# Gate rows of the mLSTM heads: requested in the projection stage of their pair

## The chip, the cores and the metric

The kernel runs on one core of a Trainium2 chip. The metric is the device time of one execution in microseconds (us), as a median over runs. The core's engines are TensorE (PE, matrix multiplies and transposes; its weight loads are shown as PEld), VectorE (DVE), ScalarE (ACT), GpSimd (POOL) and SyncE (SP). Each works through its own queue in order and waits on semaphores for the others. All loads and stores of this kernel are issued by SP and carried out by 16 DMA engines.

## What is computed

Two layers of a bidirectional encoder run over two request groups of 256 and 512 tokens with shared weights, width 1024. Each layer has a mixer stage with three groups of heads (A: dilated attention, 4 heads; B: mLSTM, 4 heads; C: grouped-query attention, 8 heads), a cross attention into 256 memory tokens, and a gated FFN with a convolution. The part that matters here is B. Cut down, and for one direction:

```
g  = gates of the head                      # input gate ig, forget gate lf = log_sigmoid(...)
b  = cumsum(lf)                             # over the tokens
logw[l, s] = b[l] - b[s] + ig[s]            # s <= l (forward); the backward scan has s >= l
w_intra = exp(logw - m[l]) * (q[l] . k[s])
h[l] = sum_s w_intra v[s] / max(|sum_s w_intra|, exp(-m[l]))
```

The kernel computes each mLSTM head as a full attention within its stream: for a block of 128 queries it needs, along the keys, the row `ig - b` of the forward and of the backward direction, the same for all queries. These are the gate rows. They are added to a triangular mask in the diagonal block, put through an exponential with a bias by query, and multiplied with the scores.

## The kernel before, in words

Activations are kept transposed, features on the 128 partitions and the 768 tokens of both streams along the free axis (`T` = 768; `STREAMS` is first tokens 256 to 767, then 0 to 255). Values are float32, split into a high and a low float32r part for the matrix multiplies. A large buffer `f_all` (`arena_f` in the rows), `F_COLS` = 14 x 768 = 10752 float32 columns, is handed out in pieces by an `Arena`: it gives the columns that have been free for longest, and the tile framework makes a new user of columns wait for the last user. `arena_r` is the same for float32r values. Softmax tiles (`palloc`, 512 columns each) and nearly all intermediate results of a mixer stage come from `arena_f`.

In the mixer stage (`mixers`) each head group has a projection (`c_q`, `b_proj`, `a_proj`) and an attention (`c_attn`, `b_attn`, `a_attn`). The helper `ahead(first, second)` writes the projection of the next group with a low priority and the attention of the present one with a high priority, so that a scheduler fills the attention's gaps with the next projection. The scheduler sets the order in every engine's queue when the program is built. The order of the groups is C (two groups of four heads), B (two pairs of heads, `pb` = 0 and 1), A (two pairs).

`gates` computes the gate rows of all four B heads and both directions in 36 partitions and stores them to DRAM (`scr_g`, line 560). `b_proj(pb)` projects the pair's queries and keys, convolves them, stacks them by DMA (`stacks`, line 362) and projects the values (`v_proj`). `b_attn(pb)` goes over the two heads `e` of the pair and the two streams; for each it takes a buffer `gbt` of 2n columns (1024 or 512), loads the two gate rows from `scr_g` into it, repeated over all partitions (line 729), and calls `attend` with the softmax `b_soft`. For each block of 128 queries `b_soft` adds the mask to the diagonal part (DVE, the tile that reads `arena_f,cs`), takes up to four exponentials (ACT, lines 748 to 752) and multiplies them with the scores from PSUM while summing (DVE, line 754); PE's score products (lines 375, 376) refill a PSUM bank that line 754 has read, and its transposes of the weights (line 387) read the softmax tile, after which the tile's columns are free.

There are 16 such gate-row loads: 2 heads x 2 streams x 2 pairs x 2 layers. In the FFN the same `f_all` is split anew: the first 7168 columns hold weight sums, the rest (3584 columns) the working tiles of one step.

Of the kernel before, what the change touches and what calls it, by code (L numbers as in the profile page):

```python
# [30 lines left out]
T = 768  # L31
# [3 lines left out]
STREAMS = ((256, 512), (0, 256))  # L35
# [9 lines left out]
R_COLS = 18 * 768  # L45
S_COLS = 4 * 512
PREP = 7 * 512
F_COLS = 14 * 768
N_PAR = 143

K_ID, K_TRI, K_IND = 0, 128, 384
# [57 lines left out]
def trunk_kernel(ctx, tc, xT, memT, w_in, w_out, w_xq, w_xkv, w_xo, w_up, w_dn, w_dnt, par, fin_g, cst, fmk, tabs,  # L109
                 out_p, out_s):  # L110
    nc = tc.nc
    V, A, G, PE, SY = nc.vector, nc.scalar, nc.gpsimd, nc.tensor, nc.sync
# [12 lines left out]
    ap = ctx.enter_context(tc.tile_pool(name="ap", bufs=1))  # L125
    f_all = ap.tile([128, F_COLS], F32, name="arena_f")
    af = Arena(f_all, F_COLS)
    r_all = ap.tile([128, R_COLS + S_COLS], F32R, name="arena_r")
# [26 lines left out]
    scr_g = nc.dram_tensor("scr_g", (DEPTH, 36, T), F32, kind="Internal").ap()  # L155

    def tt(out, a, b, op):
        V.tensor_tensor(out, a, b, op=op)  # L158

    def stt(out, a, s, b, op0, op1):  # L160
        V.scalar_tensor_tensor(out=out, in0=a, scalar=s, in1=b, op0=op0, op1=op1)  # L161
# [78 lines left out]
    def proj(src, xh, xl, evac, streams=STREAMS, sub="", chunks=None):  # L240
        chunks = chunks or wload8(src, sub)
        for c0, n in streams:
            ps = ps_tile(n)
            mm_chunks(ps[:, :n], chunks, xh, xl, c0, n)
            evac(ps[:, :n], c0, n)
# [76 lines left out]
    def split(src, hi, lo, n, scale=None, sub="sp"):  # L322
        hi_op(pick("h" + sub, "A"), hi[:, :n], src[:, :n], scale)
        if scale is None:
            tt(lo[:, :n], src[:, :n], hi.bitcast(F32)[:, :n], ALU.subtract)
        else:
            stt(lo[:, :n], src[:, :n], scale, hi.bitcast(F32)[:, :n], ALU.mult, ALU.subtract)
# [9 lines left out]
    def v_tokens(zv, nt, vv, site):  # L337
        for c0, n in (STREAMS if nt == 6 else ((0, 512),)):
            ps = small_ps(site, "vps")
            m = n // 128  # L340
            j0 = c0 // 128
            for i in range(m):
                PE.transpose(ps[:, i * 128:(i + 1) * 128], zv[:, c0 + i * 128:c0 + (i + 1) * 128], ident)
            for e in range(2):
                src = ps[:, :n].rearrange("p (i h d) -> p i h d", h=2, d=64)[:, :, e]
                a, b = 64 * e, 64 - 64 * e
                A.copy(vv[e][:, j0:j0 + m, a:a + 64], src)
                tt(vv[e][:, j0:j0 + m, b:b + 64], src, vv[e].bitcast(F32)[:, j0:j0 + m, a:a + 64], ALU.subtract)
# [164 lines left out]
    def mixers(l, xt, x_dram, stats):  # L513
# [7 lines left out]
        def ev_to(z, name):  # L521
            return ev_scaled(z, rbc, name)
# [91 lines left out]
        def v_proj(t):  # L614
            zv = ft()
            proj(w_in[l, t], xh, xl, ev_to(zv, "v%d" % t), sub="w_v%d" % t)
            vv = [rtl(), rtl()]
            v_tokens(zv, 6, [tok(v) for v in vv], "v%d" % t)
            af.free(zv)
            return vv  # L620
# [56 lines left out]
        def stacks(qq, kk):  # L677
            out = []
            qf, kf = qq.bitcast(F32), kk.bitcast(F32)
            for e in range(2):  # L680
                r = slice(64 * e, 64 * e + 64)
                qs, K = rtl(), rtl(2 * T)
                load_stack(qs, [(0, qf[r, :T]), (64, qf[r, T:])])
                load_stack(K, [(0, kf[r]), (64, kf[r])])
                out.append((qs, K))
            ar.free(qq, kk)
            return out

        def b_proj(pb):
            parts = []  # L690
            for j in range(2):
                ti = 6 + 2 * j + pb
                ci = 2 * j + pb
                u = af.tile(771)
                G.memset(u[:, 0:1], 0.0)
                G.memset(u[:, 257:258], 0.0)
                G.memset(u[:, 770:771], 0.0)

                def ev_c(ps, c0, n, u=u):
                    o = c0 + (2 if c0 else 1)  # L700
                    tt(u[:, o:o + n], ps, rbc[:, c0:c0 + n], ALU.mult)
                proj(w_in[l, ti], xh, xl, ev_c, sub="w_b%d%d" % (pb, j))
                t = af.tile(769)
                w = lambda r, ci=ci: pr[:, l, C_BW + 4 * r + ci:C_BW + 4 * r + ci + 1]
                A.activation(t, u[:, 1:770], ACT.Identity, scale=w(1), bias=pr[:, l, C_BB + ci:C_BB + ci + 1])
                stt(t, u[:, 0:769], w(0), t, ALU.mult, ALU.add)
                stt(t, u[:, 2:771], w(2), t, ALU.mult, ALU.add)
                th = af.tile(769)
                A.activation(th, t, ACT.Tanh)
                z = u[:, 0:T]  # L710
                stt(z[:, 0:256], th[:, 0:256], 1.0, t[:, 0:256], ALU.add, ALU.mult)
                stt(z[:, 256:768], th[:, 257:769], 1.0, t[:, 257:769], ALU.add, ALU.mult)
                hl = rtl(2 * T)
                split(z, hl[:, :T], hl[:, T:], T, sub="b_sp%d" % pb)
                af.free(u, t, th)
                parts.append(hl)
            sts = stacks(*parts)
            return sts, v_proj(10 + pb)

        def b_attn(pb, sv):  # L720
            SITE[0] = "b%d" % pb
            sts, vv = sv
            for e in range(2):
                qs, K = sts[e]
                hd = 2 * pb + e
                for c0, n in STREAMS:
                    gbt = af.tile(2 * n)
                    gb = gbt.rearrange("p (d k) -> p d k", d=2)
                    SY.dma_start(out=gb, in_=scr_g[l, hd:hd + 33:32, c0:c0 + n].partition_broadcast(128))
                    attend(qs, c0, n // 128, K[:, :T], K[:, T:], c0, n, tok(vv[e]), c0 // 128, e, yt[5 + pb], c0,  # L730
                           b_soft(gb, c0, n, hd))
                    af.free(gbt)
                ar.free(qs, K, vv[e])

        def b_soft(gb, c0, n, hd):
# [127 lines left out]
        def f1():  # L863
            r = c_q(1)
            gates()
            return r
        qc1 = ahead(f1, lambda: c_attn(0, qc0), "0")
        sb0 = ahead(lambda: b_proj(0), lambda: c_attn(1, qc1), "1")
        sb1 = ahead(lambda: b_proj(1), lambda: b_attn(0, sb0), "2")
        sa0 = ahead(lambda: a_proj(0), lambda: b_attn(1, sb1), "3")  # L870
        def fa():
            r = a_proj(1)
# [98 lines left out]
    def ffn(l, xt, stats):  # L971
        _, rbc = stats
        rf = Arena(r_all, R_COLS + S_COLS, T)
        fp = Arena(f_all[:, :2 * PREP], 2 * PREP)
        fw = Arena(f_all[:, 2 * PREP:], F_COLS - 2 * PREP)
        fs = Arena(f_all[:, PREP:2 * PREP], PREP)
        ftm = Arena(f_all[:, 2 * PREP:], F_COLS - 2 * PREP)
        tg = f_all[:, F_COLS - T:]
        gf = pr[:, l, C_FFN:C_FFN + 8]
# [388 lines left out]
```

## Time and profile before

| | |
|---|---|
| time, median of 3 runs | 2231.02 us (2229.93 to 2237.94) |
| the profiled execution: its time, its span | 2230.71 us, 2228.8 us |
| PE busy, PE weight loads busy | 91%, 81% |
| DVE busy, ACT busy | 86%, 46% |
| mean granted TensorE clock | 0.951 of full speed |
| chain that ended last: PE, DVE, ACT, DMA | 69%, 18%, 5%, 5% |
| mixer stage, first layer: 245 to 300 us | PE 40.06, DVE 43.80 us busy, clock 0.75 |
| mixer stage, first layer: 300 to 350 us | PE 39.94, DVE 39.11 us busy, clock 0.86 |
| mixer stage, second layer: 1320 to 1370 us | PE 38.23, DVE 32.46 us busy, clock 0.90 |
| FFN main loop, first layer: 640 to 1050 us | PE 404.17, DVE 389.01 us busy, clock 1.00 |

A busy PE is not PE at its peak: matrix multiplies overlap in the records. The granted clock is the share of full speed at which the chip let TensorE run; 0.50 is the lower of its two levels, 1.2 of 2.4 GHz. The chain is found by going back from the last instruction, at each step to what released it. A waiting time is idle time of an engine directly before an instruction, put down to the last of the things that it waited for.

### The profile page before, as it was taken

The numbers are of one execution on the slowest core, as the hardware profiler recorded it, in microseconds if no ns is written. First come the engines' busy times: TensorE is split into PE (matmuls) and PEld (weight loads), VectorE is DVE, ScalarE is ACT, GpSimd is POOL, SyncE is SP. The second block draws the span as 40 slices with busy tenths as digits, with TensorE's granted clock in tenths as the row PEclk, the third lists the DMA queues.
The fourth block names the chain that finished last, engine by engine and source line by source line (L and its number), as shares of the span: only waits on it lengthen the run. The fifth ranks groups of instructions, "written<-read, shape, count | busy, mean of one in ns | idle before, by whom it ended". The sixth has DMA issues, their size and how long they took to land.

```text
span 2228.8 us, 31329 instructions
## 1 busy us (share of the span) xinstructions
PE 2036.8 (91%) x11256; PEld 1801.0 (81%) x11256; DVE 1925.8 (86%) x4191; ACT 1031.6 (46%) x2030; POOL 2.3 (0%) x28
## 2 busy tenths in 40 slices
PE   7989788898889999999999897898988999999996
PEld 5877667677769999999888775776867899999995
DVE  8787788778899999999978777878789999999997
ACT  4256645546633333333444675465565333333342
POOL 0000000000000000000000000000000000000000
PEclk8989888899999999999999897999998999999998
DMA  5422341434212222222245133443422222222211
GB/s 202 121 59 71 97 110 48 130 114 119 86 52 86 68 67 75 67 67 69 89 150 139 41 80 89 103 113 121 125 76 66 86 67 67 74 69 66 67 38 67
DMA packets 64684, 195.16 MB, mean 88 GB/s; under 512 B 8264, under 2 KB 11592, under 8 KB 63760
## 3 DMA queue, kind: packets, MB, share of 16 engines
q1 hardware_dynamic: 64528, 193.15, 29.7%
q8 instruction: 89, 1.46, 0.3%
q14 instruction: 67, 0.55, 0.1%
HBM read 150.17 MB, written 10.71 MB: 72 GB/s over the span
## 4 chain that ended last, share of the span: by engine, by line
PE 69%; DVE 18%; ACT 5%; DMA 5%; issue 2%; SPq 1%; DVEq 0%; ACTq 0%
PE rps L1066 9%; PE rps L1068 9%; PE rps L1067 9%; DVE arena_f L158 5%; PE rps L1109 5%; PE rps L1110 4%; PE rps L1111 4%; PE prS L213 4%; PE prS L214 4%; PE prS L215 4%; DVE arena_r L158 2%; PE t L387 2%; PE prP L213 2%; DVE xall L158 2%; DVE arena_f L161 2%
## 5 line engine op out<-in xcount | busy, mean ns | idle before, releaser
L183 ACT CAST wh<-arena_f 128x512 fp32r<-128x512 f32 x280 | 170.7, 620 | 286.3 <-PE rps L1067 231.3
L158 DVE TENSOR_TENSOR arena_f<-arena_f 128x512 f32<-128x512 f32 (+3 forms) x381 | 272.8, 733 | 19.2 <-DMA arena_f<-arena_f 8.4
L183 ACT CAST wh<-wr 128x512 fp32r<-128x512 f32 x268 | 165.0, 620 | 260.3 <-PE rps L1067 105.0
L158 DVE TENSOR_TENSOR wl<-wr,wh 128x512 fp32r<-128x512 f32 x288 | 197.5, 688 | 37.2 <-ACT wh L183 35.5
L1066 PE MATMUL rps<-xha,wh 128*128 128x384 f32 x640 | 218.7, 342 | 7.7 <-DVE arena_f L158 4.5
L1068 PE MATMUL rps<-xha,wl 128*128 128x384 f32 x640 | 213.5, 340 | 6.3 <-DVE wl L158 6.2
L1067 PE MATMUL rps<-xla,wh 128*128 128x384 f32 x640 | 217.6, 340 | 0.1
L158 DVE TENSOR_TENSOR xall<-rps,xall 128x512 f32<-128x512 f32 (+1 forms) x384 | 198.4, 554 | 14.7 <-PE rps L1111 5.6
L1109 PE MATMUL rps<-arena_r,wh 128*128 128x512 f32 (+1 forms) x608 | 202.8, 340 | 1.6 <-DVE xall L158 1.6
L1110 PE MATMUL rps<-arena_r,wh 128*128 128x512 f32 (+1 forms) x608 | 200.9, 338 | 0.0
L213 PE MATMUL prS<-xha,wh 128*128 128x512 f32 x480 | 191.4, 402 | 5.5 <-DVE arena_f L158 1.9
L214 PE MATMUL prS<-xla,wh 128*128 128x512 f32 x480 | 191.6, 400 | 1.3 <-DVE xla L158 1.2
L158 DVE TENSOR_TENSOR wl<-arena_f,wh 128x512 fp32r<-128x512 f32 x280 | 189.7, 687 | 2.5 <-ACT wh L183 2.3
L215 PE MATMUL prS<-xha,wl 128*128 128x512 f32 x480 | 190.5, 398 | 0.0
L158 DVE TENSOR_TENSOR arena_f<-rps,arena_f 128x384 f32<-128x384 f32 x280 | 151.7, 555 | 33.9 <-PE rps L1068 29.9
L1111 PE MATMUL rps<-arena_r,wl 128*128 128x512 f32 (+1 forms) x608 | 177.9, 338 | 0.0
L1066 PE MATMUL rps<-arena_r,wh 128*128 128x384 f32 x480 | 163.0, 340 | 0.8 <-ACT wh L183 0.8
L1067 PE MATMUL rps<-arena_r,wh 128*128 128x384 f32 x480 | 161.9, 337 | 0.0
L1068 PE MATMUL rps<-arena_r,wl 128*128 128x384 f32 x480 | 156.0, 339 | 0.7 <-DVE wl L158 0.7
L158 DVE TENSOR_TENSOR arena_r<-t,arena_r 128x512 fp32r<-128x512 f32 x184 | 125.0, 687 | 27.9 <-ACT arena_r L183 26.6
L213 PE MATMUL prP<-xha,wh 128*128 128x256 f32 x480 | 141.8, 295 | 4.8 <-DVE arena_f L158 1.8
L387 PE MATMUL t<-cs,arena_f 128*128 128x128 f32 x736 | 127.9, 292 | 18.2 <-DVE arena_r L158 8.1
(211 smaller groups left out, 4971.4 us busy)
## 6 DMA issues: line engine op xcount, KB each, us to landing
arena_f<-in_w_up SPq DMA_DIRECT2D x80, 512.0 KB
wr<-in_w_in SPq DMA_DIRECT2D x42, 512.0 KB
wr<-in_w_dn SPq DMA_DIRECT2D x40, 512.0 KB
wr<-in_w_out SPq DMA_DIRECT2D x32, 512.0 KB
arena_r<-arena_r SPq DMA_DIRECT2D x32, 384.0 KB
arena_r<-arena_r SPq DMA_DIRECT2D x48, 192.0 KB
xall<-in_xT SPq DMA_DIRECT2D x8, 768.0 KB
arena_r<-arena_r SPq DMA_DIRECT2D x64, 96.0 KB
```

Source lines behind the costliest of these rows:

```text
L158: V.tensor_tensor(out, a, b, op=op)
L183: A.copy(out, a)
L213: PE.matmul(ps, h[:, j], xh[i][:, c0:c0 + n], start=i == 0, stop=False)
L214: PE.matmul(ps, h[:, j], xl[i][:, c0:c0 + n], start=False, stop=False)
L215: PE.matmul(ps, lo[:, j], xh[i][:, c0:c0 + n], start=False, stop=i == tot - 1)
L387: PE.transpose(t[:, j * n + i * 128:j * n + (i + 1) * 128], ptiles[i][:, (kb + j) * 128:(kb + j + 1) * 128], ident)
L1066: PE.matmul(ps, h[:, k], x[k], start=k == 0, stop=False)
L1067: PE.matmul(ps, h[:, k], x[4 + k], start=False, stop=False)
L1068: PE.matmul(ps, lo[:, k], x[k], start=False, stop=k == 3)
L1109: PE.matmul(ps, h[:, m], hh[i][:, c], start=k == 0 and not tail, stop=False)
L1110: PE.matmul(ps, h[:, m], hlo[i][:, c], start=False, stop=False)
L1111: PE.matmul(ps, lo[:, m], hh[i][:, c], start=False, stop=i == b - 1)
```

## The change

The loads of the gate rows move from `b_attn` to the end of `b_proj` of the same pair. There is one buffer of 2T = 1536 columns for each head, which takes both streams, instead of one buffer for each stream; it is freed when `b_attn` is through with the head. `arena_f` grows from 14 x 768 to 18 x 768 = 13824 columns, and to make room the scratch for dynamic DMA in SBUF is set to 1024 bytes. Shapes, number and sources of the loads and all arithmetic stay as they are.

```diff
@@ -45,7 +45,7 @@
 R_COLS = 18 * 768
 S_COLS = 4 * 512
 PREP = 7 * 512
-F_COLS = 14 * 768
+F_COLS = 18 * 768
 N_PAR = 143
 
 K_ID, K_TRI, K_IND = 0, 128, 384
@@ -715,21 +715,28 @@
                 af.free(u, t, th)
                 parts.append(hl)
             sts = stacks(*parts)
-            return sts, v_proj(10 + pb)
+            vv = v_proj(10 + pb)
+            rows = []
+            for e in range(2):
+                hd = 2 * pb + e
+                gbt = af.tile(2 * T)
+                for c0, n in STREAMS:
+                    gb = gbt[:, 2 * c0:2 * c0 + 2 * n].rearrange("p (d k) -> p d k", d=2)
+                    SY.dma_start(out=gb, in_=scr_g[l, hd:hd + 33:32, c0:c0 + n].partition_broadcast(128))
+                rows.append(gbt)
+            return sts, vv, rows
 
         def b_attn(pb, sv):
             SITE[0] = "b%d" % pb
-            sts, vv = sv
+            sts, vv, rows = sv
             for e in range(2):
                 qs, K = sts[e]
                 hd = 2 * pb + e
                 for c0, n in STREAMS:
-                    gbt = af.tile(2 * n)
-                    gb = gbt.rearrange("p (d k) -> p d k", d=2)
-                    SY.dma_start(out=gb, in_=scr_g[l, hd:hd + 33:32, c0:c0 + n].partition_broadcast(128))
+                    gb = rows[e][:, 2 * c0:2 * c0 + 2 * n].rearrange("p (d k) -> p d k", d=2)
                     attend(qs, c0, n // 128, K[:, :T], K[:, T:], c0, n, tok(vv[e]), c0 // 128, e, yt[5 + pb], c0,
                            b_soft(gb, c0, n, hd))
-                    af.free(gbt)
+                af.free(rows[e])
                 ar.free(qs, K, vv[e])
 
         def b_soft(gb, c0, n, hd):
@@ -1351,7 +1358,7 @@
     from concourse.bass_utils import run_bass_kernel_spmd as _run
 
     a = _layout({k: np.asarray(v) for k, v in inputs.items()})
-    nc = _bacc.Bacc("TRN2", target_bir_lowering=False, num_devices=1)
+    nc = _bacc.Bacc("TRN2", target_bir_lowering=False, num_devices=1, dynamic_dma_scratch_size=1024)
     arrays, args = {}, []
     for name in _ORDER:
         v = np.ascontiguousarray(a[name])
```

The scheduler sets the order anew. Lines behind the edit are 7 higher: the exponentials of lines 748, 749, 750 and 752 are 755, 756, 757 and 759 in the new program, and the gate-row loads are line 725.

SP's queue in the first layer, from the store of the gates (`scr_g<-arena_f`) on; `wr` is a weight tile, `arena_r<-arena_r` a stack load, `arena_f<-scr_g` a gate-row load of pair 0. Before:

```order
L560 DMA scr_g<-arena_f 36x768
L177 DMA wr<-in_w_in 128x1024 x2
L362 DMA arena_r<-arena_r 64x768 x2
L177 DMA wr<-in_w_in 128x1024
L362 DMA arena_r<-arena_r 64x1536 x4
L362 DMA arena_r<-arena_r 64x768 x2
L177 DMA wr<-in_w_in 128x1024 x2
L362 DMA arena_r<-arena_r 64x768 x2
L177 DMA wr<-in_w_in 128x1024
L729 DMA arena_f<-scr_g 128x2x256
L729 DMA arena_f<-scr_g 128x2x512
```

After:

```order
L560 DMA scr_g<-arena_f 36x768
L725 DMA arena_f<-scr_g 128x2x256 x2
L177 DMA wr<-in_w_in 128x1024 x2
L362 DMA arena_r<-arena_r 64x768 x2
L725 DMA arena_f<-scr_g 128x2x512 x2
L362 DMA arena_r<-arena_r 64x1536 x4
L177 DMA wr<-in_w_in 128x1024
L362 DMA arena_r<-arena_r 64x768 x2
```

The four loads of pair 0 moved from behind all projections of the pair to between the store and the pair's stack loads.

SP's queue in the first layer, later. Before, in `b_attn` of pair 1: its gate-row loads, with the stack loads of the first A pair in between:

```order
L729 DMA arena_f<-scr_g 128x2x512
L362 DMA arena_r<-arena_r 64x768
L729 DMA arena_f<-scr_g 128x2x512
L177 DMA wr<-in_w_in 128x1024
L362 DMA arena_r<-arena_r 64x768
L729 DMA arena_f<-scr_g 128x2x256
L362 DMA arena_r<-arena_r 64x768
L362 DMA arena_r<-arena_r 64x1536 x2
L362 DMA arena_r<-arena_r 64x768
L362 DMA arena_r<-arena_r 64x1536 x2
```

After, from the weights of `b_proj` of pair 1 on, up to the tables and the mask of the first A pair (`in_tabs`, `in_fmk`):

```order
L177 DMA wr<-in_w_in 128x1024 x2
L725 DMA arena_f<-scr_g 128x2x512
L362 DMA arena_r<-arena_r 64x768 x2
L725 DMA arena_f<-scr_g 128x2x512
L725 DMA arena_f<-scr_g 128x2x256
L177 DMA wr<-in_w_in 128x1024
L725 DMA arena_f<-scr_g 128x2x256
L362 DMA arena_r<-arena_r 64x1536 x4
L362 DMA arena_r<-arena_r 64x768 x2
L784 DMA arena_f<-in_fmk 128x896
L526 DMA arena_f<-in_tabs 128x768 x2
```

The four loads of pair 1 moved from among the stack loads of the A pair to among those of their own pair, ahead of the A pair's tables.

ACT's queue in the first layer, where the exponentials of `b_attn` of pair 0 stand (`arena_f<-arena_f,colm`); what each waits for is in brackets, by engine or DMA queue. Before, from the first of them on:

```order
L183 COPY xall<-yps 64x512 [waits PE_49]
L748 ACTIVATE arena_f<-arena_f,colm 128x128 [waits DMAHW2_49,Activation_49]
L183 CAST arena_r<-t 128x512 [waits PE_49]
L183 CAST arena_r<-t 128x512 [waits DVE_49,PE_49]
L183 COPY xall<-yps 64x256 [waits PE_49]
L752 ACTIVATE arena_f<-arena_f,colm 128x384 [waits DMAHW3_49]
L748 ACTIVATE arena_f<-arena_f,colm 128x128
L752 ACTIVATE arena_f<-arena_f,colm 128x256
L748 ACTIVATE arena_f<-arena_f,colm 128x256
L752 ACTIVATE arena_f<-arena_f,colm 128x128
L748 ACTIVATE arena_f<-arena_f,colm 128x384
L749 ACTIVATE arena_f<-arena_f,colm 128x128 [waits DVE_49]
```

After, in the same stage (`arena_f,den<-s` is an exponential of the C heads):

```order
L755 ACTIVATE arena_f<-arena_f,colm 128x128 [waits PE_49]
L183 CAST arena_r<-t 128x512 [waits PE_49]
L183 COPY xall<-yps 64x256 [waits PE_49]
L756 ACTIVATE arena_f<-arena_f,colm 128x128 [waits PE_49]
L755 ACTIVATE arena_f<-arena_f,colm 128x256 [waits PE_49,Activation_49]
L709 ACTIVATE arena_f<-arena_f 128x769 [waits DVE_49]
L183 CAST arena_r<-t 128x512 [waits PE_49,Activation_49]
L428 ACTIVATE arena_f,den<-s,m_2114,rq_1002 128x256 [waits DVE_49]
L428 ACTIVATE arena_f,den<-s,m_2114,rq_1002 128x256
L757 ACTIVATE arena_f<-arena_f,colm 128x128 [waits DVE_49]
L756 ACTIVATE arena_f<-arena_f,colm 128x128 [waits PE_49]
L755 ACTIVATE arena_f<-arena_f,colm 128x384 [waits PE_49]
```

Before, the exponentials stand in one block behind the gate-row loads (DMAHW). After, they are spread among the work of the C heads, and several wait for PE, that is for transposes that free their columns.

## Rows read from the trace of the kernel before

**Rows 1.** Page, part 1: busy us, share of the span, instructions.

```profile
PE 2036.8 (91%) x11256; PEld 1801.0 (81%) x11256; DVE 1925.8 (86%) x4191; ACT 1031.6 (46%) x2030; POOL 2.3 (0%) x28
```

**Rows 2.** Chain that ended last: start us, us, what; pieces in `b_attn`, first layer.

```profile
257.28 9.16 DMA arena_f<-scr_g
...
324.17 9.96 DMA arena_r<-arena_r
```

**Rows 3.** Timeline of SP: start us, us, line, operation, out<-in; both layers.

```profile
144.11 0.38 SPq L560 DMA_DIRECT2D scr_g<-arena_f  x1
162.11 9.61 SPq L177 DMA_DIRECT2D wr<-in_w_in  x2
...
373.78 0.70 SPq L784 DMA_DIRECT2D arena_f<-arena_f  x1
...
1239.47 0.32 SPq L560 DMA_DIRECT2D scr_g<-arena_f  x1
...
1461.74 0.71 SPq L784 DMA_DIRECT2D arena_f<-arena_f  x1
```

**Rows 4.** Timeline of DVE in the `b_attn` stages; in brackets idle us before, releaser.

```profile
257.35 1.43 DVE L158 TENSOR_TENSOR arena_f<-arena_f,cs 128x256 f32<-128x256 f32 x4 [1.72 <-DMA arena_f<-scr_g]
260.93 0.69 DVE L158 TENSOR_TENSOR arena_r<-t,arena_r 128x512 fp32r<-128x512 f32 x1 [2.15 <-ACT arena_r L183]
...
266.46 1.43 DVE L158 TENSOR_TENSOR arena_f<-arena_f,cs 128x256 f32<-128x256 f32 x4 [3.78 <-DMA arena_f<-scr_g]
...
328.93 0.76 DVE L158 TENSOR_TENSOR arena_f<-arena_f,cs 128x256 f32<-128x256 f32 x2 [3.34 <-DMA arena_f<-scr_g]
...
334.64 0.42 DVE L158 TENSOR_TENSOR arena_r<-vps,arena_r 128x256 fp32r<-128x256 f32 x1 [2.42 <-ACT arena_r L347]
...
1360.16 1.43 DVE L158 TENSOR_TENSOR arena_f<-arena_f,cs 128x256 f32<-128x256 f32 x4 [8.13 <-DMA arena_f<-scr_g]
...
1380.92 1.10 DVE L158 TENSOR_TENSOR arena_f<-arena_f,cs 128x256 f32<-128x256 f32 x3 [1.53 <-DMA arena_f<-scr_g]
...
1426.27 1.10 DVE L158 TENSOR_TENSOR arena_f<-arena_f,cs 128x256 f32<-128x256 f32 x3 [2.39 <-DMA arena_f<-scr_g]
```

**Rows 5.** Timeline of PE: the long gaps in the `b_attn` stages.

```profile
260.95 0.50 PE L395 MATMUL yps<-arena_r 128*128 128x512 f32 x1 [4.08 <-ACT arena_r L183]
...
270.42 0.79 PE L375 MATMUL s<-arena_r 128*128 128x512 f32 x1 [6.24 <-DVE dn L754]
...
331.33 0.55 PE L375 MATMUL s<-arena_r 128*128 128x256 f32 x1 [5.93 <-DVE dn L754]
...
1363.60 0.80 PE L375 MATMUL s<-arena_r 128*128 128x512 f32 x1 [8.26 <-DVE dn L754]
...
1428.94 0.69 PE L387 MATMUL t<-cs,arena_f 128*128 128x128 f32 x2 [5.97 <-DVE arena_f L172]
```

**Rows 6.** Stretches: length, busy us of PE, PEld, DVE, ACT, POOL, clock, DMA share, GB/s.

```profile
262.00:288.00 26.00, 17.34 (x49) 11.11 (x49) 21.96 (x122) 13.52 (x38) 0.00 (x0) 0.50 0.28 65
...
1360.00:1386.00 26.00, 16.14 (x44) 10.23 (x45) 23.23 (x126) 10.66 (x31) 0.00 (x0) 0.51 0.16 34
```

**Rows 7.** Waits, whole span: engine, line <- waited for: us in total, times, longest.

```profile
DVE arena_f L158 <- DMA arena_f<-scr_g: 26.8, 10, 8.1
...
DVE arena_f L158 <- PE t L387: 3.9, 3, 3.4
...
ACT arena_f L749 <- PE t L387: 3.6, 1, 3.6
...
ACT arena_f L748 <- PE t L387: 3.0, 3, 1.7
```

**Rows 8.** Stretches, as in rows 6: where gate-row waits didn't stop PE.

```profile
350.00:360.00 10.00, 10.00 (x65) 8.79 (x63) 7.16 (x24) 4.73 (x12) 0.00 (x0) 1.00 0.33 88
...
1320.00:1330.00 10.00, 10.00 (x61) 8.76 (x60) 6.14 (x13) 4.95 (x12) 0.00 (x0) 1.00 0.64 170
```

**Rows 9.** Waits of PE in the FFN main loop, 650 to 1050 us.

```profile
PE rps L1068 <- DVE wl L158: 4.0, 3, 2.1
```

## Prediction

> **What bounds the kernel now.** I read the page's busy shares first: TensorE (PE) is busy for 91% of the span and VectorE (DVE) for 86%, so no engine has much slack and a gain can only come out of stretches in which both stand [rows 1]. Then I looked for such stretches around the gate rows. The chain that ended last runs through gate-row loads: the one requested at 257.28 us takes 9.16 us to land [rows 2]. The order of events is in the SP rows: in layer 0 the gates are written to `scr_g` at 144.11 us [rows 3], yet the loads that read them back are requested only when `b_attn` begins, more than a hundred microseconds later. The DVE timeline shows what that costs: in each of the four `b_attn` stages (two pairs, two layers) the first mask additions wait for a load, with idle times of 1.72, 3.78, 3.34, 8.13, 1.53 and 2.39 us [rows 4]. PE stands at the same places, because the score banks aren't emptied: 4.08 and 6.24, then 5.93, 8.26 and 5.97 us [rows 5]. After the longest gap of each layer PE's granted clock is 0.50 and 0.51, its lower level of 1.2 GHz, for 26 us [rows 6]. In those two stretches DVE is busy for 21.96 and 23.23 us; most of what is missing there is its own wait for the rows. So after each gap DVE's softmax work is the limit, and PE, though slow, waits for it.
>
> **Part 1: the gate rows are requested earlier.** The number of loads (16), their bytes and the arithmetic stay the same. The order listings show where they go. In layer 0 the loads of pair 0 now follow the store of the gates within a few queue entries, a whole projection before their use; those of pair 1 are issued while `b_attn` of pair 0 begins. A load that took up to 9.16 us [rows 2] then has tens of microseconds of other work over it, so its waits go.
>
> What they are worth is counted in two ways. *By DVE*: pair 0 of layer 0 loses 1.72 and 3.78 us of waits for the rows, and 2.15 us in which DVE waited for a cast that stood behind the waiting exponentials in ScalarE's (ACT's) queue: 7.65 us. Pair 1 of layer 0 loses 3.34 us, and 2.42 us behind it, where a cast waited for a stack load that took 9.96 us [rows 2], having been issued in between two gate-row loads (the third pair of order listings shows it): 5.76 us. Layer 1 loses 8.13, 1.53 and 2.39 us: 12.05 us. Together 7.65 + 5.76 + 12.05 = 25.5 us [rows 4]. The whole trace has 26.8 us of DVE waits for these loads [rows 7]; of those, 20.9 us are in my sum (the other 4.57 us in it are the cast and the stack load). The remaining 5.9 us I price at nothing: the larger of them lie in 1320 to 1330 and 350 to 360 us, where PE is busy for 10.00 of 10 us [rows 8]. *By PE*: the five gaps are 4.08 + 6.24 + 5.93 + 8.26 + 5.97 = 30.5 us [rows 5].
>
> I take DVE's 25.5 us. When the rows are there, the next thing late is DVE's stream of multiply-reduces and scalings, which runs nearly without a gap from 266 to 293 us already; the stage shrinks by what DVE stood, not by what PE stood. [...]
>
> **Part 2: the queue and the waits the loads now meet.** On SP's queue the loads of pair 0 stand ahead of weight loads (`wr`), which before the change are issued 18 us after the store, at 162.11 us [rows 3], since they wait for DVE to free their buffer; the queue has room there. The loads of pair 1 stand ahead of stack loads that are needed one stage later. I price this at nothing; if that cover is gone, a weight load comes later by one arena wait of the requests.
>
> **Part 3: the larger arena and the tighter room in it.** The arena grows by 3072 columns, but the gate rows of one pair now hold 3072 columns from `b_proj` to the end of `b_attn`, and of two pairs 6144 while pair 0 is worked on. What is left for softmax tiles then is 13824 - 6144 = 7680 columns, against 10752 - 1024 = 9728 before. The new program shows what follows: of the 160 exponentials, 28 instead of 14 wait for a PE transpose that frees their columns, and of the 48 mask additions 17 instead of 4. The trace of before has such waits: 3.6 us once and 3.0 us in three for the exponentials, so 6.6 / 4 = 1.65 us each; 3.9 us in three, 1.3 us each, for DVE [rows 7]. The bounds are therefore nothing (each stands beside other work of ACT, which is busy for 46% only) and 14 x 1.65 + 13 x 1.3 = 40.0 us (all on the path). I take nothing: these instructions are queued far ahead of the scores that they are multiplied with, before the last attention of the C heads is through, while before they came right in front of the multiply. In the FFN the arena's second part grows from 3584 to 6656 columns, more than two sets of its tiles; its main loop keeps its order on PE and DVE, and PE's waits there are about 4 us in 400 [rows 9], so nothing to -4 us per layer; I take nothing. The smaller scratch for dynamic DMA I price at nothing: the DMA view names SP's hardware queue as the issuer of every load and store, and no row shows a use of the scratch.
>
> **Part 4: other order.** The scheduler sets the whole mixer stage anew. What a mere change of order is worth can be read off the two layers, which do the same work in different orders: from the store of the gates to the second pair's rotary copies, 373.78 - 144.11 = 229.7 us in layer 0 and 1461.74 - 1239.47 = 222.3 us in layer 1 [rows 3]. So 7.4 us per layer in either direction, 15 us for both; it widens the range and has no sign.
>
> **The sum.** The profiled execution took 2230.7 us (span 2228.8 us plus 1.9 us around it), which is 0.3 us under the median of 2231.0 us. 2230.7 - 25.5 = 2205.2 us, or 1.1% faster; with the swing of order, 2190 to 2220 us.
>
> **Rivals.**
> *A, the clock comes back too.* The gaps bring the clock to its lower level; without them PE would stay at 2.4 GHz. The row for it is 0.50 in 262 to 288 us, after PE had stood for 4.08 and 6.24 us [rows 5, 6]. PE's work at that level in the two longest stretches is 17.34 + 16.14 = 33.5 us, half of which is 16.7 us. If the early exponentials also let the multiply-reduces spread into the stage before, DVE isn't the limit, and the gain is PE's 30.5 + 16.7: 2183.5 us. Against it: DVE was the limit in just these stretches. The Trainium skill ("TensorE: Matmul & The Clock Gate", section "HAM oscillation — how this bites in real kernels") describes this: an idle wait for a DMA throttles TensorE, and the work after it pays double; the trace agrees on the fall. By that rule alone the return is counted whether or not another engine limits.
> *B, arena waits replace the gate waits.* Half of the 40.0 us of part 3 lies on the path: 2205.2 + 20.0 = 2225.2 us, within half a per cent of before. For it: the 14 + 13 added waits stand in the program, and ACT's queue is in order.
> *C, slower.* ACT's queue in the `b_attn` stages, mostly pair 0 of layer 0: exponentials that now stand early in the queue wait for columns, and behind them stand the casts that PE needs. All 40.0 us on the path give 2205.2 + 40.0 = 2245.2 us. It decides the sign from 25.5 / 40.0, about two thirds of these waits on the path, and passes half a per cent from (25.5 + 11.2) / 40.0, nine tenths.
> *D, nothing happens,* because the requests wait for arena columns until the same moment: 2230.7 us. Against it: in the order listing pair 0's requests of both layers stand right behind the store.
>
> **How the numbers follow.** My forecast (2190 to 2220 us) 0.62; A 0.12; B 0.14; C 0.08; D 0.04. The range should hold 8 in 10: the forecast's stretch and most of A and B, so 2183 to 2228 us, leaving out C, D and the far side of A. Half a per cent is 11.2 us, about what a measurement of this kernel tells from no change; faster means under 2219.9 us. Faster: A, and nearly all of the forecast: 0.73. Same: B, D and a little of the forecast's upper end: 0.19. Slower: C: 0.08.
>
> **What would show it.** In the profile of after, waits of DVE and ACT for loads from `scr_g` under 5 us in all, and these loads gone from the chain. DVE above nine tenths busy in the `b_attn` stages. PE's gaps of 4 to 8 us there gone or under 3 us; the stretch from store to rotary copies some 13 us shorter in each layer, on average. The FFN loops as long as before, to 2 us. If waits of ACT for transposes rise from 6.6 us to over 25 us, B or C is at work; if the clock stays near 1.0 through the stage and the stretch shrinks by 25 us per layer, it is A. My forecast is wrong if the gate waits go and the stretches don't shrink.

## The result and the profile after

The changed kernel takes 2200.9 us (median; 2199.2 to 2206.7), the kernel before beside it 2234.5 us: a ratio of 0.985, with a 95% interval of 0.982 to 0.989. That is 1.5% faster, three times the half a per cent that a measurement of this kernel can tell. The prediction was 2205 us, in the range 2183 to 2228 us. The profiled execution has a span of 2197.3 us, 31.5 us less than before. One run of `arena_16`, a kernel of the experiments below, took 3935 us where its other five took 2209 to 2216 us, and is left out of its figures.

Part 1 of the page of after (engine, busy us, share of the span, instructions), to be read against [rows 1]:

```profile
PE 2032.2 (92%) x11256; PEld 1801.6 (82%) x11256; DVE 1924.4 (88%) x4191; ACT 1032.9 (47%) x2030; POOL 2.3 (0%) x28
```

Busy times moved by 4.6 us at most (PE 2036.8 to 2032.2), so what went is nearly all idle time. Where it went shows when both spans are cut at the same places in PE's work: a point in the FFN of layer 0, one behind that FFN, and the same two in layer 1. The stretches of before (columns as in [rows 6]):

```profile
0.00:701.05 701.05, 605.93 (x3241) 506.49 (x3242) 570.88 (x1425) 361.40 (x776) 1.25 (x16) 0.92 0.36 101
701.05:1132.44 431.39, 429.53 (x2428) 405.39 (x2427) 408.50 (x695) 172.21 (x271) 0.00 (x0) 1.00 0.22 72
1132.44:1807.24 674.80, 600.47 (x3314) 510.04 (x3313) 558.57 (x1391) 347.19 (x750) 1.05 (x12) 0.93 0.35 99
1807.24:2228.80 421.56, 400.87 (x2279) 379.06 (x2277) 387.88 (x683) 150.77 (x233) 0.00 (x0) 0.98 0.20 64
```

And of after:

```profile
0.00:685.98 685.98, 605.44 (x3247) 508.24 (x3248) 571.10 (x1425) 360.30 (x776) 1.31 (x16) 0.92 0.36 103
685.98:1117.13 431.15, 427.61 (x2418) 403.90 (x2417) 408.79 (x695) 172.81 (x271) 0.00 (x0) 1.00 0.23 71
1117.13:1775.83 658.70, 598.46 (x3317) 510.46 (x3316) 556.76 (x1391) 348.94 (x750) 0.98 (x12) 0.94 0.36 101
1775.83:2197.30 421.47, 400.74 (x2279) 378.99 (x2277) 387.76 (x683) 150.86 (x233) 0.00 (x0) 0.98 0.21 64
```

The two mixer stages give everything: 701.05 to 685.98 is 15.1 us, 674.80 to 658.70 is 16.1 us. The FFN stretches stay as they were, to 0.2 us. PE's and DVE's work in the mixer stages is the same to 2 us, and the clock is the same to 0.01.

The requests, on SP's timeline of after (L725 is the gate-row load, L791 the rotary copy; columns as in [rows 3]):

```profile
142.81 0.38 SPq L560 DMA_DIRECT2D scr_g<-arena_f  x1
153.46 0.90 SPq L725 DMA_DIRECT2D arena_f<-scr_g  x2
...
174.89 6.25 SPq L725 DMA_DIRECT2D arena_f<-scr_g  x2
...
352.98 0.70 SPq L791 DMA_DIRECT2D arena_f<-arena_f  x1
...
1232.29 0.32 SPq L560 DMA_DIRECT2D scr_g<-arena_f  x1
...
1340.77 3.97 SPq L725 DMA_DIRECT2D arena_f<-scr_g  x3
...
1431.19 0.70 SPq L791 DMA_DIRECT2D arena_f<-arena_f  x1
```

The first two loads of pair 0 of layer 0 are requested 11 us behind the store and the other two 32 us behind it; one of the four was requested at 257.28 us before [rows 2], 113 us behind the store. The row at 1340.77 us is the exception: three of the four loads for pair 1 of layer 1 are issued only there. They stand behind four stack loads in SP's queue, the first of which had waited 8.7 us for DVE; one of the three waited another 1.1 us, for PE. One is the only gate load left on the chain, where the prediction wanted none. SP's timeline and the piece of the chain:

```profile
1336.11 4.57 SPq L362 DMA_DIRECT2D arena_r<-arena_r  x4
1340.77 3.97 SPq L725 DMA_DIRECT2D arena_f<-scr_g  x3
```

```profile
1344.29 7.73 DMA arena_f<-scr_g
```

The waits over the whole span, to be read with [rows 7]. Two more lines of before:

```profile
ACT arena_f L752 <- DMA arena_f<-scr_g: 35.0, 11, 9.0
...
PE s L375 <- DVE dn L754: 24.8, 9, 8.3
```

And after:

```profile
PE s L375 <- DVE dn L761: 16.4, 12, 3.5
...
ACT arena_f L755 <- DMA arena_f<-scr_g: 7.1, 1, 7.1
...
DVE arena_f L158 <- DMA arena_f<-scr_g: 2.0, 1, 2.0
...
ACT arena_f L759 <- PE t L387: 0.8, 1, 0.8
```

DVE's waits for gate rows fell from 26.8 to 2.0 us. ACT's, which before were 35.0 us in eleven at one line, are one of 7.1 us. Together that is 9.1 us, more than the 5 us that the prediction had set as a sign. The exponentials' waits for PE transposes, on which rivals B and C rested, did not rise: 0.8 us where [rows 7] have 3.6 and 3.0. What PE waits for at the score banks is still DVE (L761 is the multiply-reduce), but in twelve waits of at most 3.5 us (the prediction said under 3), where the longest of before was 8.26 [rows 5].

Stretches of after: the first four are those in which pair 0 of layer 0 is worked on, the last two lie in the `b_attn` stages of layer 1:

```profile
250.00:260.00 10.00, 7.86 (x34) 5.42 (x34) 9.87 (x35) 7.95 (x21) 0.00 (x0) 0.83 0.00 0
260.00:270.00 10.00, 6.00 (x20) 3.46 (x20) 9.91 (x54) 7.16 (x21) 0.00 (x0) 0.88 0.81 184
270.00:280.00 10.00, 7.98 (x27) 5.83 (x27) 9.90 (x49) 5.08 (x14) 0.00 (x0) 0.50 0.20 42
280.00:290.00 10.00, 6.57 (x26) 4.88 (x25) 10.00 (x49) 3.51 (x11) 0.00 (x0) 0.67 0.37 125
...
1340.00:1370.00 30.00, 19.94 (x83) 14.23 (x84) 25.91 (x133) 12.48 (x32) 0.00 (x0) 0.72 0.49 131
1400.00:1420.00 20.00, 13.63 (x51) 9.66 (x51) 19.91 (x98) 10.27 (x26) 0.00 (x0) 0.66 0.53 118
```

In pair 0 of layer 0 DVE is busy for 39.68 of 40 us, PE for 28.40. In [rows 6] DVE had 21.96 of 26. So DVE is the next thing late there, as the prediction said, and PE's clock still falls to 0.50, now with PE waiting for DVE instead of waiting with DVE for the rows. In layer 1 the late loads leave DVE at 25.91 of 30 us in 1340 to 1370 us, under the nine tenths that the prediction had set as a sign; in 1400 to 1420 us it has 19.91 of 20.

### The profile page after: what moved, and what is told of

Same layout as the page of the kernel before. It is cut to its first block, busy times and chain, and to the rows that moved or that the text cites. A ratio compares the mean times of both kernels' runs of the same rounds, so it can differ in the third digit from the quotient of the medians.

```text
span 2197.3 us, 31315 instructions
## 1 busy us (share of the span) xinstructions
PE 2032.2 (92%) x11256; PEld 1801.6 (82%) x11256; DVE 1924.4 (88%) x4191; ACT 1032.9 (47%) x2030; POOL 2.3 (0%) x28
## 4 chain that ended last, share of the span: by engine, by line
PE 70%; DVE 21%; ACT 4%; DMA 3%; issue 2%; SPq 1%; DVEq 0%; ACTq 0%
PE rps L1075 8%; PE rps L1073 8%; PE rps L1074 8%; DVE arena_f L158 5%; PE rps L1116 5%; PE rps L1117 5%; PE rps L1118 5%; PE prS L213 4%; PE prS L214 4%; PE prS L215 4%; DVE arena_r L158 3%; DVE arena_f L161 2%; DVE xall L158 2%; PE t L387 2%; DVE wl L158 2%
## 5 line engine op out<-in xcount | busy, mean ns | idle before, releaser
L158 DVE TENSOR_TENSOR xall<-rps,xall 128x256 f32<-128x256 f32 (+1 forms) x384 | 198.8, 554 | 15.9 <-PE rps L1196 5.1
L387 PE MATMUL t<-cs,arena_f 128*128 128x128 f32 x736 | 128.0, 291 | 13.6 <-DVE arena_r L158 8.3
```

What stands on the lines that cost most here:

```text
L387: PE.transpose(t[:, j * n + i * 128:j * n + (i + 1) * 128], ptiles[i][:, (kb + j) * 128:(kb + j + 1) * 128], ident)
```

## Experiments

The theory was that the waits for gate rows, counted on DVE, were on the path and that requesting them early takes them off. Its rival was that the gain is the larger arena, or only the new order that the scheduler made of the whole stage. Twelve kernels were run, each with runs of the kernel before on the same chip. The summary first; "DVE waits" are its waits for gate rows in the profiled execution.

| kernel | requests | arena (x 768) | median us | ratio to before, 95% | DVE waits us |
|---|---|---|---|---|---|
| before | late | 14 | 2233 to 2234 | 1 | 26.8 |
| changed | early | 18 | 2200.9 | 0.985 (0.982 to 0.989) | 2.0 |
| arena_only | late | 18 | 2215.8 | 0.992 (0.991 to 0.993) | 19.7 |
| arena_16 | late | 16 | 2209.9 | 0.990 (0.988 to 0.992) | 18.6 |
| late_both | late, own buffers | 18 | 2217.0 | 0.993 (0.991 to 0.994) | 25.7 |
| early_14 | early | 14 | 2196.7 | 0.984 (0.982 to 0.986) | none |
| early_16 | early | 16 | 2211.7 | 0.990 (0.988 to 0.992) | none |
| early_17 | early | 17 | 2206.0 | 0.988 (0.986 to 0.990) | 5.3 |
| no_load | none | 14 | 2199.8 | 0.985 (0.984 to 0.986) | none |
| short_before | late, short | 14 | 2217.5 | 0.993 (0.991 to 0.995) | 8.1 |
| short_arena | late, short | 18 | 2204.8 | 0.987 (0.985 to 0.990) | 6.3 |
| dve_less | early | 18 | 2189.6 | 0.980 (0.979 to 0.982) | 2.3 |
| act_scale | early | 18 | 2192.1 | 0.981 (0.979 to 0.983) | 2.6 |
| act_14 | early | 14 | 2188.6 | 0.981 (0.978 to 0.983) | none |

All but before and short_before also have the smaller scratch, and no run has it alone. In the program of before it changes addresses only, no order and no wait. Two traces with the smaller scratch start in the order of before, and in the same time. PE's first 888 matrix products and transposes are the same in before and early_14, and the last of them starts at 195.36 and at 195.62 us; in no_load it is the first 1022, up to 221.53 us in before and 221.18 us there. So nothing shows that the scratch counts.

**No gate loads.** The kernel before, with one constant tile `g_fix` of zeros in place of the rows, and with the smaller scratch.

```diff
+    g_fix = ap.tile([128, 1024], F32, name="g_fix")
+    nc.gpsimd.memset(g_fix, 0.0)
 ...
-                    gbt = af.tile(2 * n)
-                    gb = gbt.rearrange("p (d k) -> p d k", d=2)
-                    SY.dma_start(out=gb, in_=scr_g[l, hd:hd + 33:32, c0:c0 + n].partition_broadcast(128))
+                    gb = g_fix[:, 0:2 * n].rearrange("p (d k) -> p d k", d=2)
```

> The kernel before (arena 14 x 768) without the gate loads: the softmax of the mLSTM heads reads one constant tile of zeros instead of the rows, so the 16 loads and their arithmetic's data are left out and all instructions of the compute engines stay. It prices the gate waits at zero. Theory 1 by VectorE's count of the waits: 2234 - 26 to 2234 - 28, so 2206 to 2209 us; by TensorE's count 2234 - 30.5 = 2203 us; if the clock comes back too, 2187 us. Theory 2: within half a per cent of before, 2226 us or more.

2199.8 us: 33.8 us under the runs of before at 2233.6, a little more than either count and about what the change gives. It lies between the figure by TensorE's count and that with the clock. So without any wait for gate rows the old arena is enough. The rival of order isn't out by this: the scheduler ordered the stage anew here too.

**The arena alone, and the request early without it.**

```diff
 # arena_only, arena_16: the kernel before with
-F_COLS = 14 * 768
+F_COLS = 18 * 768        # arena_16: 16 * 768
 ...
-    nc = _bacc.Bacc("TRN2", target_bir_lowering=False, num_devices=1)
+    nc = _bacc.Bacc("TRN2", target_bir_lowering=False, num_devices=1, dynamic_dma_scratch_size=1024)
 # early_14, early_16, early_17: the changed kernel with
-F_COLS = 18 * 768
+F_COLS = 14 * 768        # early_16: 16 * 768, early_17: 17 * 768
```

> The kernel before with the larger float arena (18 x 768 columns) and the smaller scratch, the gate rows still requested in b_attn. Theory 1 (the gain is the earlier request): the waits for gate rows stay, so within half a per cent of before, 2226 to 2240 us by the runs of before at 2234. Theory 2 (the gain is the room in the arena, and the new order that it gives): most of the 33 us is here already, 2200 to 2212 us.

> The changed kernel with the arena at its old 14 x 768 columns: the requests are early, but 3072 columns fewer are left for softmax tiles while two pairs' rows are held (4608 in all). Theory 1: the gate waits go as in the changed kernel, and the added waits for columns lie beside other work, 2198 to 2210 us. Theory 2: no gain, or a loss by waits of the exponentials for columns, 2225 to 2250 us.

The early request without the larger arena gives 36.9 us, in the order that it got, as much as the whole change; that ends just below theory 1's range. The arena alone gives 17.8 us, which neither theory had. Its waits for gate rows are still long, in the whole-span view:

```profile
ACT arena_f L752 <- DMA arena_f<-scr_g: 21.3, 8, 4.0
...
DVE arena_f L158 <- DMA arena_f<-scr_g: 19.7, 10, 4.7
...
ACT arena_f L748 <- DMA arena_f<-scr_g: 10.9, 4, 4.3
```

DVE's are 7.1 us shorter than before, which does not explain 17.8 us. The other sizes were run to see whether the size counts or the order.

> The kernel before with an arena of 16 x 768 columns, the rows still requested in b_attn; 14 gave 2234 and 18 gave 2216 us. Theory a (more columns let the late requests go out sooner and one by one): between the two, 2219 to 2230 us, and a first request of each pair earlier than before. Theory b (18 was a lucky order, the size means nothing): 2230 us or more, or below 2216.

> The changed kernel (early requests) with an arena of 16 x 768 columns, between the changed kernel's 18 and the 14 that gave 2196.7 us. Theory 1 (the early request takes the waits away, and the room only shifts the order): no wait for gate rows above 5 us in all, and 2192 to 2207 us, with no trend in the arena's size. Rival (fewer columns hurt, and 14 was a lucky order): 2207 to 2220 us.

> The changed kernel with an arena of 17 x 768 columns: a fourth order of the early requests, after 14 (2196.7 us), 16 (2211.7) and 18 (2200.9). If the scatter of these is the order's and the early request is worth the same in each, 2195 to 2213 us with no gate waits above 8 us in all; a time outside of it would mean that the arena's size has an effect of its own.

Late requests give 2234, 2210 and 2216 us at 14, 16 and 18; early ones 2197, 2212, 2206 and 2201 us at 14, 16, 17 and 18. Neither rises or falls steadily with the size, so the order counts more than the size. arena_16 came out as theory b had it, below 2216 us. early_16 missed theory 1's range and lies in its rival's (2207 to 2220 us). That fewer columns hurt a little, with 14 a lucky order, isn't excluded by the early times from 16 to 18; but 14 lies 15 us under 16, so the order can outweigh it. At 16 early and late are the same within their spread, so in that pair of orders the early request gained nothing. early_17 lies in its range of time, but DVE's 5.3 us and ACT's 5.8 us of gate waits are more than the 8 us it was given. In early_16 there is no wait for gate rows at all; what PE stood for instead shows among its waits:

```profile
PE t L387 <- DVE arena_r L158: 22.7, 16, 3.3
...
PE s L375 <- DVE dn L761: 19.6, 11, 9.1
PE rps L1112 <- DVE arena_r L158: 11.1, 1, 11.1
...
PE s L375 <- DMA arena_r<-arena_r: 10.2, 2, 5.1
```

Transposes that wait for a DVE subtraction, score products that wait for DVE's multiply-reduce, a stack load that comes late, one wait of 11.1 us in the FFN: none of them is a wait for gate rows. So one order of the early requests differs from another by up to 15 us (2196.7 to 2211.7), and one of the late requests by up to 24 us. The means are 2203.8 us early and 2219.8 us late, of four and three orders; with so few and so scattered orders, their difference of 16 us is no price of the early request.

**Own buffers, but late.** The changed kernel with the loop over the pair's two heads moved into a function `gate_rows`, which is called at the start of `b_attn`.

```diff
+            return sts, vv, gate_rows(pb) if False else None
+
+        def gate_rows(pb):
             rows = []
 ...
-            return sts, vv, rows
+            return rows
 ...
             sts, vv, rows = sv
+            rows = rows or gate_rows(pb)
```

> The changed kernel's buffers and arena, but the rows of both heads of a pair are requested at the start of b_attn. Theory 1: the rows of the first head are late as before and those of the second come early; the first waits of each stage (1.72 and 3.78, 3.34, 8.13, 1.53 us of VectorE) stay and a part of the others goes, 2214 to 2232 us. Theory 2 (own buffers and arena are what counts, not the moment): 2198 to 2208 us.

2217.0 us lies in theory 1's range, but not by its mechanism: DVE's waits fell by 1.1 us only (26.8 to 25.7). This too is another order; with nearly the same gate waits it is 16.6 us faster than that of before.

**The price of the landing with the order held.** After the scheduler had set the order of before (and that of arena_only), the 16 loads alone were cut to 8 columns of each row; every instruction, its place and its waits stayed. The values in the other columns are stale. The cut also takes away nearly all of the 6 MB that these loads move.

```diff
+    def cut(x):
+        ap = [*x.ap[:2], [1, 8]]
+        return [copy.replace(x, ap=ap, bass_ap=copy.replace(x.bass_ap, ap=ap))]
 ...
+            if type(i).__name__ == "InstDMACopy" and i.ins[0].memref == "scr_g":
+                new[k] = copy.replace(i, ins=cut(i.ins[0]), outs=cut(i.outs[0]))
```

> The kernel before, every instruction in its old order with its old waits, but each of the 16 gate loads cut to the first 8 columns of its two rows (the other columns are not loaded), so that it lands sooner. Nothing else can move, so this is the price of the loads' landing without a new order. Theory W (the waits for gate rows were on the path): a landing of 2 to 3 us in place of 4.5 to 9.2 us takes about half to two thirds of the 26.8 us of VectorE's waits, 2212 to 2221 us. Theory O (the gain of the change was the new order, and the waits lie beside other work): within 5 us of before, 2228 us or more.

> The same cut of the 16 loads in the exact order of the larger-arena kernel with late requests, which took 2215.8 us and still waits 19.7 us on VectorE and 32.2 us on ScalarE for gate rows. Theory W: 8 to 13 us less, 2203 to 2208 us. Theory O (these waits lie beside other work): 0 to 4 us less, 2212 us or more.

Both times the loads were on the path. Of short_before:

```profile
ACT arena_f L752 <- DMA arena_f<-scr_g: 14.4, 7, 5.0
...
DVE arena_f L158 <- DMA arena_f<-scr_g: 8.1, 4, 4.1
```

Of short_arena:

```profile
ACT arena_f L752 <- DMA arena_f<-scr_g: 9.2, 6, 1.9
...
DVE arena_f L158 <- DMA arena_f<-scr_g: 6.3, 5, 2.7
...
ACT arena_f L748 <- DMA arena_f<-scr_g: 2.4, 2, 2.0
```

In short_before DVE's waits fell by 18.7 us (26.8 to 8.1) and the time by 16.1 us by the ratio, whose interval gives 12 to 20 us. In short_arena they fell by 13.4 us and the time by 11.0 us (2215.8 to 2204.8). So 1 us of DVE's waits is worth 16.1 / 18.7 = 0.86 and 11.0 / 13.4 = 0.82 us of time. The profiled executions, from which the waits are read, give less: the spans fell from 2228.8 to 2215.8 us and from 2213.4 to 2205.9 us, which is 13.0 / 18.7 = 0.70 and 7.5 / 13.4 = 0.56. So the price is 0.6 to 0.9, and it holds what ACT's shorter waits and the traffic taken away give too, since these weren't tried apart. Theory O is out: late loads cost time in two orders.

**Is DVE the limit once the rows are there?**

```diff
 # dve_less: this line left out; act_scale, act_14: on ACT
-                    smul("V", p[:, d1:n], p[:, d1:n], dn[:, 1:2])
+                    smul("A", p[:, d1:n], p[:, d1:n], dn[:, 1:2])
```

> The changed kernel without the scaling of the columns past the diagonal block (32 VectorE instructions, 16 of 128, 8 of 256 and 8 of 384 columns: 16 x 0.283 + 8 x 0.343 + 8 x 0.411 = 10.6 us of VectorE; the second half of those rows stays unscaled). If VectorE is what bounds b_attn once the gate waits are gone, all of it shows: 10 us less than the changed kernel, a ratio to before of 0.980 or 0.981 against the changed kernel's 0.985. If TensorE or the waits of TensorE on other things bound it, 0 to 3 us less: 0.984 or 0.985.

> The changed kernel with those 32 scalings on ScalarE instead of VectorE. If VectorE bounds b_attn and ScalarE (busy for half of the time) hides them: 10 us less than the changed kernel, 2189 to 2193 us by runs of before at 2234. If ScalarE's queue, in order, holds the casts behind scalings that wait for VectorE's reciprocals: no gain or a loss, 2200 to 2215 us.

> Early requests, the old arena of 14 x 768 columns, and the 32 scalings past the diagonal on ScalarE, which together may beat all kernels so far. If VectorE bounds b_attn in this order too: 8 to 11 us under the 2196.7 us without it, 2186 to 2189 us. If this order, whose longest wait of TensorE for VectorE was 5.9 us, is bound by something else in more places: 2192 to 2197 us.

Taking out 32 instructions whose durations sum to 10.6 us gave 11.3 us (2200.9 to 2189.6). Giving them to ACT instead gave 8.8 us (2200.9 to 2192.1). Part 1 of the pages of dve_less and act_scale:

```profile
PE 2026.2 (93%) x11256; PEld 1800.5 (82%) x11256; DVE 1917.4 (88%) x4159; ACT 1031.4 (47%) x2030; POOL 2.3 (0%) x28
```

```profile
PE 2031.7 (93%) x11256; PEld 1803.3 (82%) x11256; DVE 1916.7 (87%) x4159; ACT 1044.5 (48%) x2062; POOL 2.3 (0%) x28
```

In act_scale ACT has 11.6 us more than in the changed kernel, DVE 7.7 us less, and the time falls: ACT's queue was no obstacle. Both together, act_14, take 2188.6 us, 8.1 us under early_14, as expected if DVE is the limit; it is the best median here, 1.9% under before by the ratio, and its interval overlaps those of act_scale and dve_less.

Less DVE work made the kernel faster in all three pairs, but the size isn't a clean price. The records of DVE overlap, so its busy time fell by 7.0 us only in dve_less (1924.4 to 1917.4), less than the time did. The order wasn't held either: about 91% to 96% of PE's instructions keep their order, which is more than between two sizes of the arena (at most 81% among the early ones), but not all. And the gain is not spread like the work, of which each layer had half. From the store of the gates to the first addition of the FFN's main loop, layer 0 takes 471.8 us in the changed kernel, 459.9 in dve_less and 460.6 in act_scale; layer 1 takes 459.8, 458.9 and 458.7 us.

## Why the prediction was right, and what it mis-sized

**The bound and the next thing late: right.** The late loads were on the path, as the two runs with the order held show. Most of the gate waits went, and behind them DVE limits `b_attn` where no load is late: 39.68 of 40 us busy in pair 0 of layer 0, and less DVE work was less time in three pairs. In layer 1 it is shown less well: DVE was at 25.91 of 30 us in one stretch, and dve_less gained about 1 us there. The Trainium skill ("Perfetto Trace Analysis", section "Identifying the Most-Contended Engine") judges TensorE by its useful work and the busy share of its weight loads, not by matmul time, and calls the engine with the highest share the most contended. By [rows 1] that is DVE (86% against 81%), and dve_less agrees.

**The 25.5 us for the waits: the right mechanism, at least 4 us too much by the best estimates.** I had counted 20.9 of the 26.8 us of gate waits in full, the other 5.9 us at nothing, and 4.57 us for a cast and a stack load behind them. With the order held, DVE's gate waits as a whole count at 0.82 to 0.86 by the medians and at 0.56 to 0.70 by the profiled spans, whatever follows them included. The 24.8 us that went (26.8 to 2.0) are worth 20 to 21 us by the medians and 14 to 17 us by the spans; the ratio's interval of short_before alone (0.65 to 1.07 per us) gives 16 to 27 us, so 25.5 us isn't excluded. Without the 4.57 us for the cast and the stack load the count would have been 20.9 us; that these were counted twice is likely, but no run took them apart. (The listing in which the stack load stands between two gate-row loads is the second pair, not the third.)

**The new order: the mis-sized term.** I gave it up to 15 us in either direction, and nothing in the sum. The medians differ by 33.6 us; less the 20 to 21 us of the waits, 12 to 13 us are left for it, or up to 20 us by the lower price. By the medians its size was within my bound. So the forecast of 2205 us came out 4 us from the result in part by luck: what it had too much for the waits stands against what it had at nothing for the order. What the sum missed is that the order of before was a poor one: each of the three other late orders was 16 us or more under it (2217.0, 2215.8 and 2209.9 us), though DVE still waited 18.6 to 25.7 us for gate rows in them. The early orders' mean is 2203.8 us, and the changed kernel lies 3 us below it. That the remainder is the order's is worked out as a difference; no run had the new order with the old waits. It also means that the count by PE's gaps (2230.7 - 30.5 = 2200.2 us), though nearest to the result, is not shown to be the better one: at a held order the gain is below even DVE's count.

**The stretch from store to rotary copies was a poor measure.** It fell from 229.7 to 352.98 - 142.81 = 210.2 us and from 222.3 to 1431.19 - 1232.29 = 198.9 us, 19.5 and 23.4 us where I had announced 13, because the copies stand elsewhere in the new order. The cuts at equal places of PE's work say 15.1 and 16.1 us.

**Rival A (the clock comes back): no.** The granted clock is 0.50 in 270 to 280 us of after, where no wait for gate rows is left. In early_14, without one wait for gate rows, the same fall stands beside a full DVE:

```profile
265.00:275.00 10.00, 5.14 (x17) 2.98 (x17) 9.92 (x48) 6.76 (x19) 0.00 (x0) 0.50 0.73 166
```

The Trainium skill ("TensorE: Matmul & The Clock Gate", section "HAM oscillation — how this bites in real kernels") ties the fall to idle waits for a DMA; these rows show it with PE idle for DVE, so removing the DMA wait gave the clock no return here: its mean over the span is 0.952, 0.951 before. Other orders had a little more: no_load 0.956 to 0.962 in its runs, where before has 0.947 to 0.952 beside it. One reading of the prediction was off: in layer 0 the clock is at 0.50 from 262 us on [rows 6], while the gap of 6.24 us ended at 270.42 us [rows 5] and so began at 264.18 us; the fall stands behind the gap of 4.08 us, not behind the longest one.

**Rivals B and C (waits for columns): no.** The 14 + 13 added waits stand in the program but hardly in the trace: 0.8 us for the exponentials. They can appear in another order: early_17 has 13.6 us of them, and took 2206.0 us. early_14, with 3072 columns fewer, isn't slower than the changed kernel. Pricing part 3 at nothing held, and the larger arena isn't needed for the gain.

**Rival D: no**, by SP's rows. Requests did wait for arena columns, up to 21.3 us (`SPq L725 <- PE t L387`: 45.2 us in five), but long before the rows were needed. The late ones, the three at 1340.77 us, were late by their place behind the stack loads; they cost ACT one wait of 7.1 us. Part 2 had priced the queue at nothing; in layer 1 it cost this wait.

**The FFN at nothing** held to 0.2 us.

## What to carry over

Price a load's wait by the engine that is the limit without it, then test the price with the order held: shrink the loads after the scheduler has run, and no instruction changes its place. Where a scheduler sets a whole stage anew, run each variant in three or four orders (a neutral size does it) before a difference of half a per cent is put down to the edit. When a wait goes and another engine is at 99% of the stage, the next gain is that engine's work: moving 10.6 us of it to a half-idle engine gave 8 to 9 us, in two pairs of orders that weren't held.

## What the runs showed that I had not expected

A good part of a late gate load's time was not its own bytes. The chain's load of 9.16 us at 257.28 us [rows 2] was issued behind four stack loads on SP's queue, and the DMA engines were full during the first half of it and busy for 0.78 in the second. SP's timeline of before, and the stretches around it:

```profile
252.26 4.92 SPq L362 DMA_DIRECT2D arena_r<-arena_r  x4
257.28 6.45 SPq L729 DMA_DIRECT2D arena_f<-scr_g  x2
```

```profile
251.84:257.28 5.44, 4.41 (x26) 3.17 (x24) 2.48 (x4) 1.83 (x4) 0.00 (x0) 1.00 0.72 183
257.28:261.86 4.58, 0.68 (x2) 0.37 (x2) 2.12 (x5) 4.51 (x12) 0.00 (x0) 0.94 1.03 222
261.86:266.44 4.58, 2.32 (x7) 1.42 (x7) 0.69 (x1) 1.87 (x6) 0.00 (x0) 0.50 0.78 184
```

In short_before a load of 8 KB, 1/64 of the bytes, still takes 6.08 us at that place, and 2.55 us at another, both on its chain:

```profile
257.13 6.08 DMA arena_f<-scr_g
...
1408.01 2.55 DMA arena_f<-scr_g
```

So 3.1 us of the 9.16 went with the bytes of the gate loads, 2.55 us is what a small load takes elsewhere, and the other 3.5 us (6.08 less 2.55) is an estimate of what the place in the queue cost, which an earlier request changes and a smaller load doesn't. In arena_only the load of the same stage takes 4.62 us, with the engines' share at 0.43 over it:

```profile
246.39 4.62 DMA arena_f<-scr_g
```

```profile
246.39:251.01 4.62, 4.62 (x26) 3.81 (x25) 2.67 (x6) 1.93 (x4) 0.00 (x0) 1.00 0.43 133
```

How much of arena_only's 17.8 us comes from such shorter landings, and how much from its order alone, stays open.
